# Small triangular inverses: two 64-row product stages put on either side of the second block's sliding-window values product

## The chip, the cores and the metric

The kernel runs on one core of a Trainium2 chip. The metric is the device time of one execution in microseconds (us). Before the change the median of three runs is 1251.22 us (1250.65 to 1251.36).

## What is computed

Two layers of a decoder trunk on 256 tokens of width 1024, all in fp32. In each layer three token mixers run on the same normalised input. The part that matters here is one step of the gated delta rule and, beside it, a sliding-window attention:

```python
def gated_delta_rule(q, k, v, g, beta):          # DN_HEADS = 4 heads of 128
    ...
    a = jnp.where(strict, jnp.einsum('bhncd,bhnsd->bhncs', k_beta, k) * decay, 0.0)
    t_mat = a + jnp.eye(C, dtype=f32)
    sol = lax.linalg.triangular_solve(t_mat, rhs, left_side=True, lower=True, unit_diagonal=True)
    ...

def sliding_window_attention(q, k, v, sinks):    # WINDOW = 128, two blocks of 128 tokens
    ...
    p = jnp.exp(s - m)
    p = p / (p.sum(-1, keepdims=True) + jnp.exp(sink - m))
    o = jnp.einsum('bnhgqk,bnkhd->bnqhgd', p.astype(v.dtype), vb)
```

After the mixers come a projection of each branch, gates, a common output projection and feed-forward stages. All of these are large matrix products whose weights (some 250 MB) stream in from memory once.

## The kernel before

**Weights.** Every weight piece of 128 x 1024 (`unit`, L110) is fetched by SyncE into a `raw` buffer (four of them), rounded by ScalarE into `whi` (a CAST) and completed by VectorE, which writes the remainder `wlo` (`split`, L125). A large product is then three TensorE matmuls (`mm3`: high by high, high by low, low by high), 128 x 512 each. There are five `whi` and five `wlo` buffers. A scheduler puts the casts at a priority of 300 instructions ahead of their place in the program.

**The small inverses.** Instead of a triangular solve the kernel inverts the two 128-row blocks (c = 0, 1) of each head by doubling: 16-row inverses on GpSimd, then `doubling` (L982 on) makes 32-row and 64-row inverses in four steps, each a group of small matmuls and a few copies on ScalarE, VectorE or GpSimd. `double` runs one step for both blocks. Two further stages make the 128-row inverse: `lower_products` (eight 64 x 64 matmuls, two ScalarE copies L1046 and L1047 into `TM`, in the trace `w`) and `upper_products` (eight 64 x 64 matmuls that read those copies, then two ScalarE multiplications L1056 into the inverse `Y`). The next user of `Y` is `rec_v0`, four 128 x 128 matmuls.

**Sliding attention.** `w_scores(tb, hh)` makes the scores and the softmax of block tb and half hh of the heads (ScalarE: L857, four exponentials L860, four multiplications L863). For the second block (tb = 1) the result must be turned. `w_leave(hh)` does this with two VectorE transposes each (L893, into `u` for hh = 0, into `bB` for hh = 1) and four GpSimd-issued DMAs to memory (L896, `tw`). `w_back` fetches it back with four GpSimd DMAs (L906, into two `pt` buffers, one for each 128 keys, each filled by one DMA of hh = 0 and one of hh = 1). `w_values(1)` multiplies both `pt` with the values: its first matmul waits for both DMAs into the first `pt`, its third for both into the second.

**What sets the order.** Large and small work is interleaved by hand with `weave` (after the n-th step of a large product, call these functions). TensorE's instructions in this part are kept in program order. ScalarE, VectorE and GpSimd are ordered by the scheduler from priorities and `issue_after` links, and at run time each executes its list strictly as it stands. The part at hand occurs once in each layer: `gates(1)`, eight steps with the doubling between them, then `branch(1)`, the projection of the sliding branch, four products of twelve matmuls.

Of the kernel before, what the change touches and what calls it, by code (L numbers as in the profile page):

```python
# [32 lines left out]
MAGIC = 0x5F3759DF  # L33
AHEAD = 300
HOLD = 4


@with_exitstack
def tile_trunk(ctx, tc, x, xT, mem, memT_, wst, lnp, memln, cvw, rows, cst, out):
    nc = tc.nc  # L40
# [21 lines left out]
    def T(pool, shape, tag, dt=F32, bufs=None):  # L62
        pool = pn if pool is pu and tag in NEAR else pool
        kw = {} if bufs is None else {"bufs": bufs}
        return pool.tile(shape, dt, tag=tag, name=nm(tag), **kw)

    def acc():
        return T(psA, [P, 512], "acc")

    def at():  # L70
        return T(psT, [P, 512], "at")

    def sm():
        return T(psS, [P, 512], "sm")
# [29 lines left out]
    def unit(w=U, dst=None, cuts=1, behind=None, parts=1):  # L104
        ahead = tc.high_priority(offset=AHEAD) if pos[0] >= 8 * P * U else nullcontext()
        raw = T(praw, [P, U], "raw")
        src = wst[pos[0]:pos[0] + P * w].rearrange("(p w) -> p w", p=P)
        pos[0] += P * w
        (ph, th), (pl, tl) = dst or ((phi, "whi"), (plo, "wlo"))
        with ahead:  # L110
            hi = T(ph, [P, U], th, F32R)
            lo = T(pl, [P, U], tl, F32R)
            for i in range(cuts):
                c = slice(i * w // cuts, (i + 1) * w // cuts)
                nc.sync.dma_start(raw[:, c], src[:, c])  # L115
                with ExitStack() as held:
                    for b in behind if isinstance(behind, tuple) else (behind,) if behind else ():
                        held.enter_context(tc.issue_after(b))
                    for j in range(c.start, c.stop, (c.stop - c.start) // parts):
                        e = slice(j, j + (c.stop - c.start) // parts)  # L120
                        newest[:] = split(hi[:, e], lo[:, e], raw[:, e])
        return hi, lo

    def split(hi, lo, src):
        return nc.scalar.copy(hi, src).ins, nc.vector.tensor_tensor(lo, src, hi.bitcast(F32), op=ALU.subtract).ins  # L125
# [3 lines left out]
    def pe(ins):  # L129

        return tc.keep_in_program_order(ins) if pinned[0] else ins

    def matmul(*a, **k):
        return pe(nc.tensor.matmul(*a, **k))  # L134
# [4 lines left out]
    def mm3(o, l, r, first, last, skip=False):  # L139
        (lh, ll), (rh, rl) = l, r  # L140
        matmul(o, lh, rh, start=first, stop=False, skip_group_check=skip)
        matmul(o, lh, rl, start=False, stop=False, skip_group_check=skip)
        matmul(o, ll, rh, start=False, stop=last, skip_group_check=skip)

    def weave(work, steps):

        for n, _ in enumerate(work, 1):
            for f in steps.get(n, ()):
                f()
# [410 lines left out]
    def mixers(l, hT, mkT, mv_, post0, post):  # L560
# [65 lines left out]
        def held(f):  # L626
            with ExitStack() as st:
                for b in late.values():
                    st.enter_context(tc.issue_after(b))
                f()  # L630
# [102 lines left out]
        TM = [T(pu, [P, 2, 4, P], f"w{2 + c}") for c in range(2)]  # L733
        AK = [T(pu, [P, 4, 2, P], f"u{12 + c}") for c in range(2)]
# [173 lines left out]
        def w_values(tb):  # L908
            if not oS:
                oS.extend(T(pu, [P, 4, S], tag, F32R) for tag in ("u6", "u7"))  # L910
            ts = slice(tb * P, (tb + 1) * P)
            pso = at()
            for kb in range(tb + 1):
                for kv in range(2):
                    hs = slice(kv * 64, kv * 64 + 64)
                    o, w = pso[hs].rearrange("p (y i x) -> p y i x", y=8, i=2), wpT[tb][kb].rearrange("p h (a i v x) -> p (h a) i v x", a=4, i=2, v=2)[:, :, :, kv]
                    matmul(o, swv[:, kb, hs], w, start=kb == 0, stop=kb == tb)
            for y in range(2):
                split(*(t[:, 2 * y:2 * y + 2, ts].rearrange("p i (a x) -> p i a x", a=4) for t in oS), pso[:, y * S:y * S + S].rearrange("p (a i x) -> p i a x", a=4, i=2))
# [42 lines left out]
        X64, X32, Y32 = (W[:, a:b].rearrange("p (c h i) -> p c h i", c=2, h=4) for a, b in ((0, 512), (512, 768), (768, 1024)))  # L962
        Y = T(pu, [P, 2, 4, P], "w1")
# [62 lines left out]
        stages = [doubling(c) for c in (1, 0)]  # L1026

        def double():
            for d in stages:
                next(d)  # L1030

        up, dn = slice(0, 64), slice(64, P)

# [5 lines left out]

        def lower_products():  # L1040

            pa, pb = (sm().rearrange("p (h c) -> p h c", h=4) for _ in range(2))
            for h in range(4):
                matmul(pa[dn, h, up], AK[0][up, h, 0, dn], X64[up, 0, h], start=True, stop=True)
                matmul(pb[up, h, dn], AK[1][dn, h, 0, up], Y[dn, 1, h, dn], start=True, stop=True)
            nc.scalar.copy(TM[0][dn, 1, :, up], pa[dn, :, up])  # L1046
            nc.scalar.copy(TM[1][up, 1, :, dn], pb[up, :, dn])  # L1047

        def upper_products():

            pa, pb = (sm().rearrange("p (h c) -> p h c", h=4) for _ in range(2))
            for h in range(4):
                matmul(pa[up, h, dn], TM[0][dn, 1, h, up], Y[dn, 0, h, dn], start=True, stop=True)
                matmul(pb[up, h, dn], X64[up, 1, h], TM[1][up, 1, h, dn], start=True, stop=True)
            for c, ps in enumerate((pa, pb)):
                nc.scalar.mul(Y[up, c, :, dn], ps[up, :, dn], -1.0)  # L1056

        def begin_inverse():

# [97 lines left out]
        def branch(n, o):  # L1157
            us = [unit(behind={1: late.get("pairs"), 2: fin.get("landed")}.get(n) if i > 1 else None) for i in range(4)]
            if not mg:
                mg.extend(T(pu, [P, D], f"u{4 + tb}") for tb in range(2))  # L1160
            gt = gts[n]
            for tb in range(2):
                ts = slice(tb * P, (tb + 1) * P)
                for j in range(2):
                    js = slice(j * 512, (j + 1) * 512)
                    ps = acc()
                    for k, (hi, lo) in enumerate(us):
                        mm3(ps, (o[0][:, k, ts], o[1][:, k, ts]), (hi[:, js], lo[:, js]), k == 0, k == 3)
                        if (n, tb, j, k) == (1, 0, 1, 2):
                            upper_products()  # L1170
                            w_values(1)
                    dst = gt[tb] if n else mg[tb]
                    late["dve"] = nc.vector.scalar_tensor_tensor(dst[:, js], gt[tb][:, js], 1.0, ps, op0=ALU.add, op1=ALU.mult).ins
                    if n:
                        with tc.issue_after(late["back"]):
                            nc.gpsimd.tensor_tensor(mg[tb][:, js], mg[tb][:, js], gt[tb][:, js], op=ALU.add)
                    yield
# [15 lines left out]
            4: [lambda: held(lambda: w_leave(1)), w_back],  # L1193
            5: [double],
            7: [double, lambda: w_values(0), lambda: held(land_v)],
            8: [lower_products, lambda: held(leave_q)]})
        weave(branch(1, oS), {
            2: [rec_v0],
            3: [rec_s1, lambda: held(land_q)],
# [51 lines left out]
    ps = sm()  # L1251
# [14 lines left out]
    for l in range(NL):  # L1266
        mT = []
        mid = memory_T(mT, l)
        if l == 0:

            mid[2] = lambda: load(cs, cst)
            more = {4: lambda *a: xres(0), 6: lambda *a: xres(1), 8: lambda *a: small()}
        post = Post(lnp[l, 0, 0], lnp[l, 0, 1], bounce=True)
        f1.rest(hT, 4, [((pu, "u0"), (pu, "u1")), ((pu, "u2"), (pu, "u3"))], post, mid, ends, {} if l else more)
        kv = memory_kv(mT, post)
        if l == 0:
            nc.scalar.activation(nea, rw[:, :, 8:12], AF.Exp)
            nc.vector.tensor_scalar(nea, nea, -1.0, None, ALU.mult)
        post2 = Post(lnp[l, 1, 0], lnp[l, 1, 1])
        mixers(l, post.hT, *kv, post, post2)  # L1280
        f2 = Ffn()
        begin(f2, post2.hT)
        last = l == NL - 1
        post = Post(lnp[l, 2, 0], lnp[l, 2, 1], last)
        f2.rest(post2.hT, 6, [((pu, a), (pu, b)) for a, b in (("u0", "u1"), ("u2", "u3"), ("u4", "u5"), ("u6", "u13"))], post, behind=post2.end)
        ends = post.end
        if not last:
            f1, hT = Ffn(), post.hT
            begin(f1, hT)
# [87 lines left out]
```

## Time and profile before

| | us |
|---|---|
| median of three runs | 1251.22 |
| the profiled execution | 1249.48 |
| its span (first to last instruction) | 1247.3 |
| TensorE busy within the span | 1236.5 |
| VectorE busy | 887.6 |
| ScalarE busy | 655.4 |
| GpSimd busy | 271.5 |

The profiled execution is 1.74 us below the median of the three runs, and 2.2 us of it lie around the span. TensorE works nearly without a pause, so the kernel gets longer or shorter by what TensorE waits for, or by what it executes; the other engines and the DMA queues count only where TensorE has to wait for them. Two stretches matter, 361 to 371 us in the first layer and 978 to 988 us in the second: they are the same instructions 617.3 us apart.

### The profile page before, as it was taken

The numbers are of one execution on the slowest core, as the hardware profiler recorded it, in microseconds if no ns is written. First come the engines' busy times: TensorE is split into PE (matmuls) and PEld (weight loads), VectorE is DVE, ScalarE is ACT, GpSimd is POOL, SyncE is SP. The second block draws the span as 40 slices with busy tenths as digits, with TensorE's granted clock in tenths as the row PEclk, the third lists the DMA queues.
The fourth block names the chain that finished last, engine by engine and source line by source line (L and its number), as shares of the span: only waits on it lengthen the run. The fifth ranks groups of instructions, "written<-read, shape, count | busy, mean of one in ns | idle before, by whom it ended". The sixth has DMA issues, their size and how long they took to land.

```text
span 1247.3 us, 18730 instructions
## 1 busy us (share of the span) xinstructions
PE 1236.5 (99%) x6812; PEld 1052.6 (84%) x6812; DVE 887.6 (71%) x1316; ACT 655.4 (53%) x976; POOL 271.5 (22%) x481
## 2 busy tenths in 40 slices
PE   9999999999999999999999999999999999999997
PEld 6888889999878888888888888899988788888886
DVE  6688567887768876665676665769869688666555
ACT  6456545656665544444455554456657644454541
POOL 1232102003751102221012220020046411122100
PEclk9999999999999999999999999999999999999999
DMA  8988866755675848886668886676566566688771
GB/s 296 320 267 279 259 228 202 239 171 179 184 242 169 269 140 257 240 242 220 220 207 241 262 255 216 215 238 207 170 192 214 177 215 213 204 243 240 242 230 74
DMA packets 83275, 276.73 MB, mean 222 GB/s; under 512 B 13776, under 2 KB 15216, under 8 KB 83184
## 3 DMA queue, kind: packets, MB, share of 16 engines
q1 hardware_dynamic: 66320, 232.40, 58.0%
q0 software_dynamic: 16720, 43.02, 12.0%
q8 instruction: 53, 0.87, 0.3%
q14 instruction: 38, 0.31, 0.1%
q10 hardware_dynamic: 144, 0.13, 0.0%
HBM read 253.77 MB, written 21.73 MB: 221 GB/s over the span
## 4 chain that ended last, share of the span: by engine, by line
PE 99%; DMA 0%; DVE 0%; SPq 0%; issue 0%; ACT 0%; DVEq 0%
PE acc L134 88%; PE at L134 4%; PE sm L134 3%; PE sm L137 1%; PE acc L332 1%; PE acc L333 1%; PE acc L335 1%; DMA raw<-in_wst_dram 0%; PE at L137 0%; DVE h L291 0%; DVE h L296 0%; SPq L115 0%; SPq L78 0%; ACT whi L125 0%; DVE bnst L277 0%
## 5 line engine op out<-in xcount | busy, mean ns | idle before, releaser
L125 DVE TENSOR_TENSOR wlo<-raw,whi 128x1024 fp32r<-128x1024 f32 (+2 forms) x405 | 486.4, 1209 | 252.1 <-ACT whi L125 249.7
L125 ACT CAST whi<-raw 128x1024 fp32r<-128x1024 f32 (+2 forms) x405 | 413.4, 1029 | 379.7 <-PE acc L134 293.6
L134 PE MATMUL acc<-whi,hT 128*128 128x512 f32 (+1 forms) x1824 | 559.9, 385 | 0.7 <-ACT whi L125 0.7
L134 PEld LDWEIGHTS acc<-whi,hT 128*128 128x128 f32 x1824 | 339.9, 188 | 70.1 <-ACT whi L125 2.7
L134 PE MATMUL acc<-wlo,hT 128*128 128x512 f32 (+1 forms) x912 | 350.1, 384 | 0.0
L134 PE MATMUL acc<-whi,u 128*128 128x512 f32 x812 | 259.0, 392 | 0.0
L134 PEld LDWEIGHTS acc<-wlo,hT 128*128 128x128 f32 x912 | 171.3, 188 | 32.9 <-DVE wlo L125 0.8
L134 PEld LDWEIGHTS acc<-whi,u 128*128 128x128 f32 x812 | 152.3, 188 | 33.8 <-issue 1.6
L362 POOL DMA_DIRECT2D tr<-t x176 | 96.0, 552 | 307.8 <-DVE t L356 307.6
L134 PE MATMUL acc<-wlo,u 128*128 128x512 f32 x406 | 158.2, 390 | 0.0
L134 PE MATMUL acc<-hT,whi 128*128 128x256 f32 x672 | 121.8, 284 | 0.0
L134 PEld LDWEIGHTS acc<-hT,whi 128*128 128x128 f32 x672 | 104.7, 192 | 0.0
L134 PE MATMUL acc<-hT,wlo 128*128 128x256 f32 x336 | 95.1, 283 | 0.0
L134 PEld LDWEIGHTS acc<-wlo,u 128*128 128x128 f32 x406 | 76.3, 188 | 15.5
L363 POOL DMA_DIRECT2D pt<-tr x44 | 24.6, 558 | 197.1 <-DMA tr<-t 143.0
L134 PEld LDWEIGHTS acc<-hT,wlo 128*128 128x128 f32 x336 | 64.4, 192 | 0.0
L353 ACT ACTIVATE t<-acc 128x256 f32<-128x256 f32 x88 | 33.4, 379 | 37.3 <-PE acc L134 37.2
L134 PE MATMUL acc<-u,u 128*128 128x512 f32 x186 | 46.4, 394 | 0.0
L354 DVE TENSOR_TENSOR t<-t,acc 128x256 f32<-128x256 f32 x88 | 36.7, 417 | 8.1 <-ACT t L353 3.8
L134 PEld LDWEIGHTS acc<-u,u 128*128 128x128 f32 x186 | 34.6, 188 | 7.5
L125 DVE TENSOR_TENSOR u<-pt,u 128x512 fp32r<-128x512 f32 x46 | 30.3, 659 | 13.2 <-ACT u L125 13.2
L125 ACT CAST u<-pt 128x512 fp32r<-128x512 f32 x46 | 28.1, 611 | 21.3 <-DMA pt<-tr 12.3
(264 smaller groups left out, 1190.4 us busy)
## 6 DMA issues: line engine op xcount, KB each, us to landing
raw<-in_wst_dram SPq DMA_DIRECT2D x409, 512.0 KB, 4.5
tr<-t POOLq DMA_DIRECT2D x176, 64.0 KB, 3.9
pt<-tr POOLq DMA_DIRECT2D x44, 256.0 KB, 5.2
raw<-in_wst_dram SPq DMA_DIRECT2D x16, 324.0 KB, 4.4
gB<-in_lnp_dram SPq DMA_DIRECT2D x6, 512.0 KB, 6.0
bB<-in_lnp_dram SPq DMA_DIRECT2D x6, 512.0 KB, 6.2
pt<-tw POOLq DMA_DIRECT2D x12, 256.0 KB, 5.6
tn<-pp POOLq DMA_DIRECT2D x16, 128.0 KB, 4.1
```

What stands on the lines that cost most here:

```text
L125: return nc.scalar.copy(hi, src).ins, nc.vector.tensor_tensor(lo, src, hi.bitcast(F32), op=ALU.subtract).ins
L134: return pe(nc.tensor.matmul(*a, **k))
L137: return pe(nc.tensor.transpose(*a))
L332: nc.tensor.matmul(ps, hT[0][:, k, ts], hi[:, c], start=k == 0, stop=False)
L333: nc.tensor.matmul(ps, hT[0][:, k, ts], lo[:, c], start=False, stop=False)
L335: nc.tensor.matmul(ps, hT[1][:, k, ts], hi[:, c], start=False, stop=k == KD - 1)
L353: act = nc.scalar.activation(t[:, :, tb, :], g, AF.Silu).ins
L354: ins = nc.vector.tensor_tensor(t[:, :, tb, :], t[:, :, tb, :], u, op=ALU.mult).ins
L362: nc.gpsimd.dma_start(d[:, :, q].rearrange("b c x -> c b x"), z[32 * q:32 * q + 32].rearrange("c (b x) -> c b x", b=4))
L363: back = nc.gpsimd.dma_start(y, d.rearrange("b c q x -> (b c) (q x)")).ins
```

## The change

The two 64-row stages are moved. `lower_products` was called after the last step of `gates(1)`; `upper_products` and then `w_values(1)` were called within the second product of `branch(1)`, before its last three matmuls. Now the order at that second place is `lower_products`, `w_values(1)`, `upper_products`, and nothing of them stands behind `gates(1)`. Apart from that, all steps of `double` and both stages get a scheduler priority of 120 instructions ahead. No instruction is added or removed.

```diff
+SOON = 120
...
         def double():
-            for d in stages:
-                next(d)
+            with tc.high_priority(offset=SOON):
+                for d in stages:
+                    next(d)
...
         def lower_products():
 
-            pa, pb = (sm().rearrange("p (h c) -> p h c", h=4) for _ in range(2))
...
+            with tc.high_priority(offset=SOON):
+                pa, pb = (sm().rearrange("p (h c) -> p h c", h=4) for _ in range(2))
...
         def upper_products():
 
-            pa, pb = (sm().rearrange("p (h c) -> p h c", h=4) for _ in range(2))
...
+            with tc.high_priority(offset=SOON):
+                pa, pb = (sm().rearrange("p (h c) -> p h c", h=4) for _ in range(2))
...
                         if (n, tb, j, k) == (1, 0, 1, 2):
+                            lower_products()
+                            w_values(1)
                             upper_products()
-                            w_values(1)
...
-            8: [lower_products, lambda: held(leave_q)]})
+            8: [lambda: held(leave_q)]})
```

TensorE's list around `w_values(1)` in the first layer. `sm` of 64x64 are the two stages, `at<-pt` is `w_values(1)`, `acc` is the large product. Before, the upper stage, the values and the large product:

```order
L134 MATMUL sm_3877<-w_469_2587,w_459_2575 64x64
L134 MATMUL sm_3878<-w_460_2576,w_468_2586 64x64
L134 MATMUL at_3889<-pt_3639,swv_2065 64x512 x2
L134 MATMUL at_3889<-pt_3640,swv_2065 64x512 x2
L134 MATMUL acc_3867<-whi_3847,u_655_3767 128x512
```

Now, the lower stage, the values and the upper stage:

```order
L135 MATMUL sm_3865<-w_468_2586,u_461_2577 64x64
L135 MATMUL sm_3866<-w_469_2587,u_462_2578 64x64
L135 MATMUL at_3877<-pt_3639,swv_2065 64x512 x2
L135 MATMUL at_3877<-pt_3640,swv_2065 64x512 x2
L135 MATMUL sm_3886<-w_469_2587,w_459_2575 64x64
L135 MATMUL sm_3887<-w_460_2576,w_468_2586 64x64
```

The lower stage has moved 21 large matmuls later, from ahead of `branch(1)` to ahead of the values, and the upper stage has moved behind the values.

The new priority also reorders ScalarE and VectorE earlier, within `gates(1)`. ScalarE's list there in the first layer: CAST `whi` are the four weight pieces of `branch(1)` (the names of one list are not those of the other), `pp_3496` is the softmax of the second block's second half, COPY `w` are copies of the doubling. Before, from the first weight cast on:

```order
L125 CAST whi_3829<-raw_3828 128x1024
L860 ACTIVATE pp_3496,sums_3508<-pp_3496,mx_3507 128x256 x2
L1154 ACTIVATE gt_3439<-acc_3441 128x512
L1019 COPY w_468_2586<-w_468_2586 32x4x32
L125 CAST whi_3835<-raw_3834 128x1024
L863 ACTIVATE pp_3496<-pp_3496,sums_3508 128x256 x4
L1008 COPY w_460_2576<-sm_3665 32x4x32 x2
L1008 COPY w_459_2575<-sm_3676 32x4x32 x2
L125 CAST whi_3841<-raw_3840 128x1024
```

Now, from the first weight cast on:

```order
L126 CAST whi_3817<-raw_3816 128x1024
L861 ACTIVATE pp_3496,sums_3508<-pp_3496,mx_3507 128x256 x4
L126 CAST whi_3823<-raw_3822 128x1024
L1009 COPY w_460_2576<-sm_3665 32x4x32 x2
L1009 COPY w_459_2575<-sm_3676 32x4x32 x2
L864 ACTIVATE pp_3496<-pp_3496,sums_3508 128x256 x3
L126 CAST whi_3829<-raw_3828 128x1024
L864 ACTIVATE pp_3496<-pp_3496,sums_3508 128x256
```

Ahead of these rows the four copies from the second doubling step, formerly spread behind them, now stand around the softmax's first small exponential (L858); the last of the four multiplications of `pp_3496` now stands behind the third weight cast instead of ahead of it.

VectorE's list at the same place, where `wlo` are the remainders of those weights and `bB` the two transposes of `w_leave(1)`. Before:

```order
L125 TENSOR_TENSOR wlo_3830<-raw_3828,whi_3829 128x1024
L861 TENSOR_TENSOR sums_3508<-sums_3508,sk_3509 128x4
L862 RECIPROCAL sums_3508<-sums_3508 128x4
L125 TENSOR_TENSOR wlo_3836<-raw_3834,whi_3835 128x1024
L893 STREAM_TRANSPOSE bB_3631<-pp_3496 128x512 x2
L656 TENSOR_TENSOR u_392_2081<-u_392_2081,kn_2083 128x512
```

Now:

```order
L126 TENSOR_TENSOR wlo_3818<-raw_3816,whi_3817 128x1024
L862 TENSOR_TENSOR sums_3508<-sums_3508,sk_3509 128x4
L863 RECIPROCAL sums_3508<-sums_3508 128x4
L126 TENSOR_TENSOR wlo_3824<-raw_3822,whi_3823 128x1024
L126 TENSOR_TENSOR wlo_3830<-raw_3828,whi_3829 128x1024
L894 STREAM_TRANSPOSE bB_3631<-pp_3496 128x512 x2
L657 TENSOR_TENSOR u_392_2081<-u_392_2081,kn_2083 128x512
```

The two transposes now stand behind the third weight remainder instead of the second. On GpSimd the eight copies of the second doubling step (L1023) now stand ahead of the four DMAs of `w_leave(0)`; the rest of its list keeps its order, and SyncE's list is unchanged. The second layer's lists show the same moves.

## Rows read from the trace of the kernel before

**Rows 1.** The page: busy us, share of the span, instructions.

```profile
PE 1236.5 (99%) x6812; PEld 1052.6 (84%) x6812; DVE 887.6 (71%) x1316; ACT 655.4 (53%) x976; POOL 271.5 (22%) x481
```

**Rows 2.** Timeline, TensorE, first layer: start us, us, engine, line, operation, [idle before].

```profile
361.22 0.39 PE L134 MATMUL acc<-whi,hT 128*128 128x512 f32 x1
361.54 0.68 PE L134 MATMUL sm<-w,u 64*64 64x64 f32 x16
362.15 0.50 PE L134 MATMUL acc<-whi,u 128*128 128x512 f32 x1
362.49 0.39 PE L134 MATMUL acc<-wlo,u 128*128 128x512 f32 x1
362.72 0.62 PE L134 MATMUL acc<-whi,u 128*128 128x512 f32 x2
...
367.14 0.68 PE L134 MATMUL sm<-w,w 64*64 64x64 f32 x16
367.75 1.94 PE L134 MATMUL at<-pt,swv 128*64 128x512 f32 x8
```

**Rows 3.** Timeline, TensorE, second layer: the same values product.

```profile
985.07 1.94 PE L134 MATMUL at<-pt,swv 128*64 128x512 f32 x8
```

**Rows 4.** Timeline, ScalarE, first layer.

```profile
345.92 0.21 ACT L857 ACTIVATE sk<-sk 128x4 f32<-128x4 f32 x1 [0.32 <-DVE sk L856]
346.68 0.60 ACT L1154 ACTIVATE gt<-acc 128x512 f32<-128x512 f32 x1 [0.56 <-PE acc L134]
...
348.73 1.04 ACT L125 CAST whi<-raw 128x1024 fp32r<-128x1024 f32 x1
349.66 0.51 ACT L860 ACTIVATE pp<-pp,mx 128x256 f32<-128x256 f32 x1
...
352.27 1.70 ACT L863 ACTIVATE pp<-pp,sums 128x256 f32<-128x256 f32 x4
354.00 1.09 ACT L1008 COPY w<-sm 32x128 f32<-32x128 f32 x4
...
356.19 0.92 ACT L1019 COPY w<-w 32x128 f32<-32x128 f32 x3
...
367.85 0.65 ACT L1056 ACTIVATE w<-sm 64x256 f32<-64x256 f32 x2 [3.54 <-PE sm L134]
```

**Rows 5.** Timeline, VectorE, first layer.

```profile
345.13 0.70 DVE L893 STREAM_TRANSPOSE u<-pp 128x512 f32<-128x512 f32 x1
...
346.43 1.18 DVE L125 TENSOR_TENSOR wlo<-raw,whi 128x1024 fp32r<-128x1024 f32 x1
...
347.60 0.48 DVE L999 TENSOR_TENSOR w<-w,sm 128x128 f32<-128x128 f32 x2
348.00 0.49 DVE L1000 STREAM_TRANSPOSE w<-w 128x128 f32<-128x128 f32 x2
...
354.00 1.31 DVE L893 STREAM_TRANSPOSE bB<-pp 128x512 f32<-128x512 f32 x2 [0.38 <-ACT pp L863]
```

**Rows 6.** Timeline, GpSimd: the last two fetches of `w_back`, first and second layer.

```profile
363.25 1.06 POOL L906 DMA_DIRECT2D pt<-tw  x2 [3.74 <-DMA tw<-bB]
...
980.32 1.06 POOL L906 DMA_DIRECT2D pt<-tw  x2 [3.49 <-DMA tw<-bB]
```

**Rows 7.** By line, issue to landing: L896 into tw<-bB; L906, first and second layer.

```profile
DMA to landing us min/median/max: 2.9/4.2/5.4
...
DMA to landing us min/median/max: 3.7/3.9/4.1
...
DMA to landing us min/median/max: 3.5/3.8/4.2
```

**Rows 8.** By stretches: stretch, length, PE, PEld, DVE, ACT, POOL busy, PEclk, DMA, GB/s.

```profile
1238.00:1240.00 2.00, 1.09 (x10) 0.89 (x8) 0.90 (x3) 0.00 (x0) 0.00 (x0) 1.00 0.00 0
1240.00:1242.00 2.00, 0.00 (x0) 0.00 (x0) 1.90 (x7) 0.29 (x1) 0.00 (x0) 0.85 0.00 0
```

**Rows 9.** Timeline, TensorE, start of the kernel: its first four matmuls.

```profile
1.52 3.78 PE L1253 MATMUL sm<-pp 128*128 128x512 f32 x4 [1.52 <-DVE pp L1250]
```

More of the change, by code (lines that the diff above doesn't have):

```diff
@@ L1040, in lower_products @@
         def lower_products():
-            pa, pb = (sm().rearrange("p (h c) -> p h c", h=4) for _ in range(2))
[L1043 to L1047, printed above, removed]
-        def upper_products():
-            pa, pb = (sm().rearrange("p (h c) -> p h c", h=4) for _ in range(2))
[L1052 to L1056, printed above, removed]
+            with tc.high_priority(offset=SOON):
+                pa, pb = (sm().rearrange("p (h c) -> p h c", h=4) for _ in range(2))
+                for h in range(4):
+                    matmul(pa[dn, h, up], AK[0][up, h, 0, dn], X64[up, 0, h], start=True, stop=True)
+                    matmul(pb[up, h, dn], AK[1][dn, h, 0, up], Y[dn, 1, h, dn], start=True, stop=True)
+                nc.scalar.copy(TM[0][dn, 1, :, up], pa[dn, :, up])
+                nc.scalar.copy(TM[1][up, 1, :, dn], pb[up, :, dn])
+        def upper_products():
+            with tc.high_priority(offset=SOON):
+                pa, pb = (sm().rearrange("p (h c) -> p h c", h=4) for _ in range(2))
+                for h in range(4):
+                    matmul(pa[up, h, dn], TM[0][dn, 1, h, up], Y[dn, 0, h, dn], start=True, stop=True)
+                    matmul(pb[up, h, dn], X64[up, 1, h], TM[1][up, 1, h, dn], start=True, stop=True)
+                for c, ps in enumerate((pa, pb)):
+                    nc.scalar.mul(Y[up, c, :, dn], ps[up, :, dn], -1.0)
         def begin_inverse():
```

## The prediction

> **What bounds the kernel now.** I read the page first, then TensorE's timeline around the moved stages, then the lists of ScalarE, VectorE and GpSimd that feed them. The page says that TensorE is busy 1236.5 us of 1247.3 [rows 1]. So the question is only what TensorE executes and what it waits for. In the timeline of the first layer [rows 2] the lower stage runs straight after the last large matmul, and the upper stage and the values product follow each other without a hole: the upper stage starts at 367.14, the values at 367.75, and the lower stage takes the same 0.61 us (361.54 to 362.15). TensorE waits for nothing here. But one of its inputs comes late: the last two fetches into `pt` are issued at 363.25 and about 363.8 [rows 6] and land 3.7 and 4.1 us later [rows 7], at 366.95 and 367.9. TensorE wants the first at 367.75 [rows 2] and the second about 0.95 later (half of the product's 1.94). The slack is 0.8 us in each case. In the second layer the fetches land at 980.32 + 3.5 = 983.82 and 980.85 + 4.2 = 985.05 [rows 6, 7], and the values start at 985.07 [rows 3]: a slack of 1.25 us for the first and 0.97 for the second. This small slack is what the change will meet.
>
> **What the move itself saves.** A 64-row stage between large matmuls costs more than its own 0.61 us. From the large matmul ahead to the stage it is 0.32 us, and the first large matmul behind holds the next up by 0.34, where two large matmuls normally follow each other at 0.23 (the 0.62 of a pair less one matmul's 0.39) [rows 2]. The lower stage therefore costs 0.32 + 0.61 + 0.34 - 2 x 0.23 = 0.81 us. Beside the values, which already pay for coming and going, it costs its 0.61. The move saves 0.20 us in each layer, 0.40 in all. It also makes TensorE arrive at the values 0.81 us earlier: `lower_products` has left its place ahead of `branch(1)`, and at the values it takes the place and the 0.61 us of `upper_products`.
>
> **The new waits in TensorE's list.** `upper_products` reads what ScalarE copies from `lower_products`. Those two copies take about as long as the two of L1056, 0.65 us, and can start some 0.71 us after the stage's start (367.85 against 367.14) [rows 2, 4]; they end 1.36 us after it, while the values alone occupy TensorE for 0.61 to 2.48 us after it. The values hide them; without that cover they would cost 0.75. Behind the upper stage stand three large matmuls (0.34 + 0.23 + 0.23) and then `rec_v0`, which reads `Y`: it is due 1.41 us after the upper stage's start, and the multiplications end 1.36 us after it. That just fits. I take it at 0 and keep 0.2 us per layer for the range. In ScalarE's list the cast of the values' first half stands ahead of those multiplications, but its input is ready before theirs.
>
> **What the priorities delay.** This is the larger part. The transposes into `bB` are the source of the late fetches: they end at 354.00 + 1.31 = 355.31, then come GpSimd's `tw` writes (up to 5.4 us to land), then the two fetches [rows 5 to 7]. In the new lists they need the fourth multiplication of `pp`, which stands behind the third weight cast, and they stand behind that cast's remainder on VectorE. I follow the new lists through the first layer with the durations of the rows. VectorE: the first transpose from 345.13 (0.70), the two L999 (0.48), the remainder (1.18), the two L1000 (0.49) [rows 5], so the first L1000 ends at about 347.7. ScalarE: the tanh of L1154 still waits for TensorE and ends at 347.28 [rows 4]. Then two copies from 347.7 at 0.31 each (0.92 for three): 348.3. The small exponential, 0.21: 348.5. Two more copies: 349.15. The first weight cast, whose successor starts 0.93 later: 350.1. Four exponentials at 0.51: 352.1. The second cast, 0.93: 353.05. Four copies, 1.09: 354.15. Three of the four multiplications, 1.28: 355.4. The third cast, 1.04: 356.45 [rows 4]. VectorE: the remainder, 1.18, to 357.65; the two transposes, 1.31, to 358.95 [rows 5]. That is 3.6 us later than before. GpSimd is free by then (its eight copies and four writes moved ahead of that time), so the whole chain of writes and fetches shifts by these 3.6 us. The weights themselves are not late: the third and fourth are read only when TensorE reaches the third and fourth quarter of a product that starts after 361. Both layers have the same lists, so I take 3.6 for each.
>
> **The sum.** First layer: the first `pt` lands at 366.95 + 3.6 = 370.55; TensorE arrives at 367.75 - 0.81 = 366.94. It waits 3.6 us; the second `pt`, at 371.5, is due then at the same moment as it lands. Second layer: 983.82 + 3.6 = 987.42 against 984.26, 3.16 us; the second `pt` lands at 988.65 against 988.37, another 0.28: 3.44 together. The waits add up to 7.05 us; less the 0.40 saved, 6.65. Nothing later gives this back, since TensorE's 99% leave no wait to absorb it.
>
> **The clock.** A wait of this length may cost once more. At the end of the kernel TensorE's last matmul ends at about 1239.1, and the granted clock, 1.00 until then, has a mean of 0.85 from 1240 to 1242 [rows 8]; between 1.00 and 0.50 (2.4 and 1.2 GHz) that puts its fall at 1241.4, 2.3 us after the work stopped. The Trainium skill states the same direction, that inactivity brings the throttle back (TensorE: Matmul & The Clock Gate, Part 1: The HAM clock gate). At the start the first four matmuls take 3.78 us [rows 9], 0.85 or more each, where four pairs of the values product with the same 512 columns take 1.94 [rows 2]: the clock is low for at least 3.8 us of work. If it falls 2.3 us into a wait of 3.5 and stays low for 3.8, some 2.6 us of work run at half speed, a loss of 1.3 us. No row shows a wait of this length between matmuls, so this is bounded by 0 and 3.8 / 2 = 1.9 us for each layer. I take one fall in the two layers, 1.3 us, because the wait is longer than 2.3 us but not by much.
>
> On the profiled execution, 1249.48 + 6.65 + 1.3 = 1257.4; it lies 1.74 below the median, so the median goes to **1259.2 us**.
>
> **The rivals.** *Not slower: quick transfers.* The price of the delay hangs on what `tw` and `pt` need to land. Of the four `tw` writes the quickest landed in 2.9 us, the slowest in 5.4 [rows 7]; in the new order they are issued later, when perhaps fewer weight transfers are under way. With 2.9 for the last write the chain is 2.5 us shorter: waits of 1.1 and 0.95 us, no fall of the clock, 2.05 - 0.4 = 1.65 more, 1252.9: no difference that can be told. It decides if the last write lands in under 3.6 us or so. Against it: the weight fetches are released by the same remainders at nearly the same times as before. The Trainium skill gives such a GpSimd-issued transfer about 2.0 us and its bytes over 436 GB/s (DMA: Bandwidth & Descriptors, Anatomy of one DMA); the estimate from that page is 2.3 us for a write of 128 KB and 2.6 for a fetch of 256 KB, by which `pt` would land ahead of TensorE and the sum would be only the 0.4 saved, 1250.8. The rows' 5.4 and 3.7 speak against that, since DMA engines are shared with the weights. *Only the move counts.* If the fourth multiplication and the transposes turn out not to gate the fetches, 1251.22 - 0.4 = 1250.8, also within the noise. Against it: the idle time of GpSimd ahead of the fetches ends with the `tw<-bB` writes [rows 6]. *Worse.* The clock falls in both layers with 1.9 each and `rec_v0` waits 0.2 each: 6.65 + 3.8 + 0.4, 1262.1.
>
> **How the numbers follow.** The forecast, both layers wait for `pt` and the clock falls at most once: 0.62 (1256 to 1260.5). Clock falls in both layers or transfers land later: 0.16 (1260.5 to 1263). Quick transfers: 0.15, of which 0.04 still over 0.2%. Only the move: 0.07, of which 0.03 for a gain that I do not see. A measurement of this kernel tells about 0.2%, 2.5 us, from no change. That gives slower 0.82, same 0.15, faster 0.03. The range leaves out the worst of the third case and most of the last two: 1254.5 to 1262.5.
>
> **What would show it.** In the profile after: a hole in TensorE of some 3.5 us just ahead of `at<-pt` in both layers, released by the DMA `pt<-tw`; the `bB` transposes ending 3.6 us later relative to the stages around them; the lower stage without a gap ahead of that hole; no wait of the upper stage on ScalarE. A granted clock below 1.00 in the stretches behind the holes shows the clock term. The prediction is wrong if the fetches land in time, if ScalarE reaches the fourth multiplication earlier than at about 356, or if `branch(1)` starts late for a weight or for the first block's values.

## The result and the profile after

| | before | after |
|---|---|---|
| median of the runs made side by side, us | 1250.93 (1249.10 to 1251.36) | 1260.01 (1259.07 to 1262.34) |
| ratio to before, 95% interval | | 1.0081 (1.0068 to 1.0093) |
| the profiled execution, us | 1249.48 | 1259.07 |
| its span, us | 1247.3 | 1257.0 |

The kernel got slower by 0.8%, some 9 to 10 us, where 1259.2 was forecast. TensorE's time by cause of waiting (us in total, times, longest) has one entry of that size, where before had none at this place:

```profile
PE at L135 <- DMA pt<-tw: 7.5, 2, 3.8
```

TensorE's timeline shows the two places. First layer, answering [rows 2] (start us, us, engine, line, operation, [idle before and what ended it]):

```profile
366.49 0.68 PE L135 MATMUL sm<-w,u 64*64 64x64 f32 x16
370.87 1.94 PE L135 MATMUL at<-pt,swv 128*64 128x512 f32 x8 [3.69 <-DMA pt<-tw]
372.74 0.68 PE L135 MATMUL sm<-w,w 64*64 64x64 f32 x16
373.35 0.50 PE L135 MATMUL acc<-whi,u 128*128 128x512 f32 x1
...
374.15 1.05 PE L135 MATMUL sm<-u,w 128*128 128x128 f32 x8
374.96 0.47 PE L135 MATMUL acc<-whi,u 128*128 128x512 f32 x1
```

Second layer, answering [rows 3]:

```profile
987.15 0.68 PE L135 MATMUL sm<-w,u 64*64 64x64 f32 x16
991.59 3.68 PE L135 MATMUL at<-pt,swv 128*64 128x512 f32 x8 [3.76 <-DMA pt<-tw]
995.20 1.12 PE L135 MATMUL sm<-w,w 64*64 64x64 f32 x16
996.25 0.79 PE L135 MATMUL acc<-whi,u 128*128 128x512 f32 x1
...
997.35 1.05 PE L135 MATMUL sm<-u,w 128*128 128x128 f32 x8
998.16 0.47 PE L135 MATMUL acc<-whi,u 128*128 128x512 f32 x1
```

From the lower stage's start to the values' start 0.61 us would be enough; it takes 370.87 - 366.49 = 4.38 and 991.59 - 987.15 = 4.44. The waits cost 3.77 and 3.83, together 7.6 us. In the second layer the values product itself takes 3.68 instead of 1.94, and from its start to the large matmul behind `rec_v0` it is 6.57 us, against 4.09 in the first layer: another 2.48 us. With the 0.4 us that the move saves, 7.6 + 2.48 - 0.4 = 9.7, the difference of the spans.

The source, as it stands in VectorE's timeline, answering [rows 5]: the `bB` transposes now end at 359.02 instead of 355.31.

```profile
356.57 1.23 DVE L126 TENSOR_TENSOR wlo<-raw,whi 128x1024 fp32r<-128x1024 f32 x1 [2.17 <-ACT whi L126]
357.72 1.30 DVE L894 STREAM_TRANSPOSE bB<-pp 128x512 f32<-128x512 f32 x2
```

ScalarE's timeline, answering [rows 4], shows why: the third weight cast, and only then the last of the four multiplications that the transposes need.

```profile
355.51 1.03 ACT L126 CAST whi<-raw 128x1024 fp32r<-128x1024 f32 x1
356.45 0.50 ACT L864 ACTIVATE pp<-pp,sums 128x256 f32<-128x256 f32 x1
```

And GpSimd, answering [rows 6]: the last two fetches are issued at 366.94 instead of 363.25, 3.69 us later.

```profile
359.31 2.31 POOL L897 DMA_DIRECT2D tw<-bB  x4 [7.04 <-DVE bB L894]
...
366.94 1.07 POOL L907 DMA_DIRECT2D pt<-tw  x2 [4.22 <-DMA tw<-bB]
...
988.08 1.07 POOL L907 DMA_DIRECT2D pt<-tw  x2 [4.36 <-DMA tw<-bB]
```

The second layer by stretches of 2 us (stretch, length, busy time of PE, PEld, DVE, ACT, POOL, then PEclk, the granted clock as a share of 2.4 GHz, DMA share, GB/s), the view of [rows 8]:

```profile
988.00:990.00 2.00, 0.00 (x0) 0.00 (x0) 0.00 (x0) 0.59 (x2) 1.85 (x4) 1.00 0.92 291
990.00:992.00 2.00, 0.41 (x2) 0.33 (x4) 0.00 (x0) 0.00 (x0) 1.01 (x1) 0.53 0.61 227
992.00:994.00 2.00, 2.00 (x6) 0.54 (x4) 0.00 (x0) 0.00 (x0) 1.26 (x3) 0.50 0.00 0
994.00:996.00 2.00, 2.00 (x18) 0.80 (x16) 0.28 (x1) 0.37 (x1) 0.97 (x2) 0.50 0.20 8
996.00:998.00 2.00, 2.00 (x16) 1.70 (x14) 0.59 (x2) 0.90 (x3) 0.00 (x0) 0.77 0.02 4
998.00:1000.00 2.00, 2.00 (x12) 1.70 (x11) 0.58 (x2) 0.59 (x1) 1.29 (x1) 1.00 0.00 0
```

And the wait of the first layer in the same view:

```profile
368.00:370.00 2.00, 0.00 (x0) 0.00 (x0) 0.00 (x0) 0.00 (x0) 1.80 (x3) 1.00 0.89 293
370.00:372.00 2.00, 1.13 (x6) 0.54 (x8) 0.00 (x0) 0.00 (x0) 0.15 (x1) 1.00 0.18 69
```

In the second layer TensorE stands still from 987.8 on. Its clock is at the upper level (1.00, 2.4 GHz) for 2.3 us of that, drops to 0.50 (1.2 GHz) at 990.1 and comes back at 996.9. These two moments follow from the means 0.53 and 0.77, and the trace's own record of the clock has them at 990.11 and 996.94. In the first layer the clock stays at 1.00 through a wait of almost the same length. The profiled execution is the shortest of the four, with a mean granted clock of 0.996 over its span; the other three have 0.993 to 0.994, so one fall need not be the usual case. Their traces were not taken.

### The profile page after: what moved, and what is told of

Read it like the earlier page. It is cut to its first block, busy times and chain, and to the rows that moved or that the text cites. A ratio compares the mean times of both kernels' runs of the same rounds, so it can differ in the third digit from the quotient of the medians.

```text
span 1257.0 us, 18726 instructions
## 1 busy us (share of the span) xinstructions
PE 1239.1 (99%) x6812; PEld 1054.5 (84%) x6812; DVE 886.0 (70%) x1316; ACT 655.4 (52%) x976; POOL 271.3 (22%) x481
## 4 chain that ended last, share of the span: by engine, by line
PE 90%; DMA 3%; DVE 2%; POOL 2%; issue 1%; ACT 1%; SPq 0%; DVEq 0%; POOLq 0%; ACTq 0%
PE acc L135 81%; PE at L135 3%; PE sm L135 2%; DMA raw<-in_wst_dram 1%; PE sm L138 1%; PE acc L333 1%; PE acc L334 1%; PE acc L336 1%; DMA tw<-bB 1%; DVE wlo L126 1%; POOL t L954 1%; DMA pt<-tw 1%; DMA w<-dr 0%; ACT whi L126 0%; POOL t L955 0%
```

## The experiments

Theory: the priority on `double` delays the `bB` transposes, so the fetches, so the values product; and where TensorE stands still that long its clock falls and some work behind runs at half speed. Rival: the new place of the two 64-row stages makes the cost. The runs below share chips and runs of before in two groups; the median of before is 1249.95 us in the first (`move_only`, `double_prio`, `fill`, `leave80`) and 1249.75 in the second. Ratios are to before; 0.001 is 1.25 us.

**The move alone** (`move_only`): the stages stand where the change puts them, no priority is raised.

```diff
-            with tc.high_priority(offset=SOON):
+            with nullcontext():
```

(at all three places)

> The stages stand where the change puts them, no priority is raised. Theory (the delayed transposes make the cost): the bB transposes end near 355.3 as before, the first pt lands near 366.95, TensorE arrives at the values 0.81 earlier (366.94) and waits 0 to 0.15 us in each layer; the clock stays at 1.00 until the end; 1250.9 - 0.4 + 0.1 = about 1250.6. Rival (the place of the stages makes the cost): holes of 3.5 us or more ahead of the values as in the changed kernel, about 1260.

Measured: 1251.26 us, ratio 1.0009 (1.0000 to 1.0018). The rival's 1260 is out: the place of the stages makes little of the cost, about a tenth. But the theory's gain of 0.3 did not come either; the ratio says a loss of about 1 us, though its interval begins at no loss at all. TensorE's timeline of the first layer shows where one can come from:

```profile
360.88 0.39 PE L135 MATMUL acc<-whi,hT 128*128 128x512 f32 x1
361.69 0.50 PE L135 MATMUL acc<-whi,u 128*128 128x512 f32 x1 [0.41 <-ACT u L126]
...
364.02 0.73 PE L135 MATMUL acc<-whi,u 128*128 128x512 f32 x2 [0.20 <-DVE u L126]
...
367.86 1.08 PE L135 MATMUL at<-pt,swv 128*64 128x512 f32 x4
369.71 1.08 PE L135 MATMUL at<-pt,swv 128*64 128x512 f32 x4 [0.77 <-DMA pt<-tw]
```

Two things that were covered before are bare in this execution. At the start of `branch(1)` the split of the first block's values (`u`) is late by 0.4 and 0.2 us; the lower stage used to lie over it. (In the changed kernel, whose lower stage is gone from there too, `branch(1)` starts in the first layer without such a wait, at 361.64.) And the second `pt` lands 0.8 us after TensorE wants it. In this execution the transposes ended at 356.16, 0.85 us later than in before, while TensorE was 0.34 earlier (360.88 against 361.22 for the last matmul of `gates(1)`, [rows 2]). The lists are the same: a weight cast on ScalarE waited 2.13 us for its weight's DMA and started at 339.42, in before 0.91 and 338.58. The whole list behind it shifted. The 0.81 us by which TensorE now arrives earlier at the values were the slack that would have taken up most of that.

**The priority alone, on `double`** (`double_prio`): the stages back at their old places, their priorities off, so that TensorE's list is that of before.

```diff
-            with tc.high_priority(offset=SOON):
+            with nullcontext():
                 pa, pb = (sm().rearrange("p (h c) -> p h c", h=4) for _ in range(2))
...
+                            upper_products()
-                            lower_products()
                             w_values(1)
-                            upper_products()
...
-            8: [lambda: held(leave_q)]})
+            8: [lower_products, lambda: held(leave_q)]})
```

(the first of these edits in both stages)

> Only the steps of double get the priority; the two 64-row stages stand where they stood before. Theory: the bB transposes end near 359, pt lands as late as in the changed kernel (370.7 and 987.4 + 4.0), TensorE arrives 0.81 later than there, so the waits are 3.77 - 0.81 = 2.96 and 3.83 - 0.81 = 3.02, 6.0 together: 1250.9 + 6.0 = 1256.9 if the clock stays at 1.00, 1259.4 if it falls once (2.5 each). Rival (the place of the stages makes the cost): waits under 0.3 us, about 1250.9.

Measured: 1259.79 us, ratio 1.0072 (1.0058 to 1.0085). So this one priority brings the loss by itself. TensorE's timeline, both layers, and VectorE's transposes:

```profile
366.59 0.68 PE L135 MATMUL sm<-w,w 64*64 64x64 f32 x16
370.53 3.68 PE L135 MATMUL at<-pt,swv 128*64 128x512 f32 x8 [3.26 <-DMA pt<-tw]
...
990.15 0.68 PE L135 MATMUL sm<-w,w 64*64 64x64 f32 x16
993.94 3.38 PE L135 MATMUL at<-pt,swv 128*64 128x512 f32 x8 [3.11 <-DMA pt<-tw]
```

```profile
356.93 1.30 DVE L894 STREAM_TRANSPOSE bB<-pp 128x512 f32<-128x512 f32 x2
```

The waits cost 3.94 - 0.61 = 3.33 and 3.79 - 0.61 = 3.18, a little more than the 3.0 expected. The clock fell not once but in both layers: both values products are slow, though both waits are shorter than the two of the changed kernel. By stretches (columns as above):

```profile
371.00:373.00 2.00, 2.00 (x6) 0.54 (x4) 0.00 (x0) 0.00 (x0) 1.46 (x3) 0.50 0.05 2
375.00:377.00 2.00, 2.00 (x11) 1.82 (x11) 1.10 (x3) 0.37 (x1) 0.40 (x1) 0.63 0.00 0
```

```profile
994.00:996.00 2.00, 2.00 (x6) 0.67 (x8) 0.00 (x0) 0.00 (x0) 1.07 (x2) 0.57 0.00 1
996.00:998.00 2.00, 2.00 (x6) 0.69 (x3) 0.24 (x1) 0.37 (x1) 1.15 (x3) 0.57 0.14 8
```

Since TensorE's list is that of before, each matmul can be set against itself. The values start 2.78 us later than in [rows 2] in the first layer and 8.87 later than in [rows 3] in the second; of the 6.09 between them 3.18 are the second wait, and 2.9 the price of the first fall. The second fall came after work had resumed and was shorter (0.50 from 994.3 to 997.7); over it the matmuls, each set against itself in before, lose 1.66 us. A fall thus has no one price here.

**The wait filled** (`fill`): the changed kernel, with matmuls added between the lower stage and the values.

```diff
-        def w_values(tb):
+        def w_values(tb, fill=None):
...
+            if fill:
+                for _ in range(15):
+                    matmul(pso, *fill, start=True, stop=True)
...
-                            w_values(1)
+                            w_values(1, (o[0][:, 0, ts], us[0][0][:, js]))
```

> The changed kernel with 15 added 128x512 matmuls between the lower stage and the values (work that is thrown away, about 15 x 0.23 = 3.4 us), so that TensorE is busy for most of the time in which it otherwise waits. Theory (the clock fell because TensorE stood still): pt lands as in the changed kernel, the added matmuls and what is left of the wait last 3.8 us together in each layer, the values product takes 1.94 in both layers, the granted clock stays at 1.00: 1250.9 - 0.4 + 7.6 = about 1258.1, 1.9 to 2.5 under the changed kernel although it executes more. Rival (the fall has another cause, or costs nothing at the end): 1260.0 with a values product of 3.7 in one layer.

Measured: 1257.89 us, ratio 1.0060 (1.0047 to 1.0072): 0.0021 or 2.6 us less than the changed kernel's ratio, for 30 matmuls more (the two intervals just overlap). TensorE's timeline of the first layer and the values of the second, then the second layer's stretches:

```profile
366.69 0.68 PE L135 MATMUL sm<-w,u 64*64 64x64 f32 x16
367.30 3.70 PE L135 MATMUL at<-whi,u 128*128 128x512 f32 x15
371.25 1.94 PE L135 MATMUL at<-pt,swv 128*64 128x512 f32 x8 [0.25 <-DMA pt<-tw]
...
992.18 1.94 PE L135 MATMUL at<-pt,swv 128*64 128x512 f32 x8
```

```profile
988.00:992.00 4.00, 4.00 (x31) 3.09 (x28) 0.25 (x1) 0.73 (x2) 2.81 (x4) 1.00 0.85 291
992.00:996.00 4.00, 3.94 (x33) 2.33 (x33) 0.77 (x2) 1.27 (x4) 2.22 (x4) 1.00 0.05 6
```

The clock stays at 1.00 and both products take 1.94. The other executions agree: all five of `fill` have a mean clock of 0.998 or 0.999, all four of the changed kernel 0.993 to 0.996. So the fall came from TensorE's standing still, and its price is a real part of the loss: about 2.5 us of the 9 to 10.

**Half of the wait filled** (`fill7`): 7 instead of 15 added matmuls.

```diff
-                for _ in range(15):
+                for _ in range(7):
```

> The changed kernel with 7 instead of 15 added 128x512 matmuls between the lower stage and the values (their products are thrown away): 7 x 0.23 = 1.6 us of the wait are filled, some 2.1 us are left in each layer. Theory (in the two records in which the clock fell ahead of the values it fell 2.3 and 2.4 us after TensorE had stopped, so a wait of 2.1 mostly ends before that): pt lands as in the changed kernel, values products of 1.94 in both layers, the clock at 1.00: as with 15, about 1257.9. Rival (any wait beyond about 1 us brings the fall): values products of 3.4 to 3.7 in a layer, 2.5 us more for each, 1260.4 or 1262.9.

Measured: 1257.61 us, ratio 1.0063 (1.0050 to 1.0076). In the profiled execution (1256.55) waits of 1.23 and 1.92 us are left, and the values take 1.98 and 1.94: no fall.

```profile
370.61 1.98 PE L135 MATMUL at<-pt,swv 128*64 128x512 f32 x8 [1.23 <-DMA pt<-tw]
...
991.50 1.94 PE L135 MATMUL at<-pt,swv 128*64 128x512 f32 x8 [1.92 <-DMA pt<-tw]
```

The median is as forecast. The rival's "any wait beyond about 1 us" is out. But the five executions go from 1255.78 to 1260.11, and the two longest (1259.37, 1260.11) lie 2 us or more above the others' middle at a mean clock of 0.997, against 0.999 and 0.998 in the two shortest; the median execution has 0.997 too. That may be a fall in one layer; their traces were not taken, so it stays open whether a wait of this length is always safe.

**The transposes brought forward again** (`leave80`): the changed kernel, and a higher priority for what the fetches hang on.

```diff
-            late["act"] = [nc.scalar.mul(pr[:, h, :nk], pr[:, h, :nk], sums[:, h:h + 1]) for h in range(4)][-1].ins
+            with (tc.high_priority(offset=LEAVE) if (tb, hh) == (1, 1) else nullcontext()):
+                late["act"] = [nc.scalar.mul(pr[:, h, :nk], pr[:, h, :nk], sums[:, h:h + 1]) for h in range(4)][-1].ins
...
-            4: [lambda: held(lambda: w_leave(1)), w_back],
+            4: [lambda: leave_soon(lambda: held(lambda: w_leave(1))), w_back],
```

(`LEAVE` is 80, `leave_soon` calls its argument at that priority)

> The changed kernel, but the four multiplications of the second softmax half and the two bB transposes are raised by 80 instructions, so that in the lists the multiplications stand ahead of the doubling's copies and of the third weight cast, and the transposes ahead of the third remainder. Theory: the transposes end near 356.15 instead of 359.0, pt lands 2.85 us earlier, waits of 0.9 (first layer) and 0.4 to 1.0 us (second), no fall of the clock: 1250.9 - 0.4 + 1.3 to 1.9 = about 1252. Rival (the wait hangs on something else, as on the eight doubling copies ahead of the writes of w_leave(0) on GpSimd, or on TensorE's earlier arrival alone): waits of 3.5 us remain, about 1260.

Measured: 1251.80 us, ratio 1.0010 (1.0002 to 1.0019). With everything else of the change in place, most of the loss is gone. VectorE's transposes in the first layer, then TensorE's values in both:

```profile
354.21 1.30 DVE L896 STREAM_TRANSPOSE bB<-pp 128x512 f32<-128x512 f32 x2 [0.39 <-ACT pp L866]
```

```profile
367.02 1.08 PE L136 MATMUL at<-pt,swv 128*64 128x512 f32 x4 [0.48 <-DMA pt<-tw]
369.19 1.08 PE L136 MATMUL at<-pt,swv 128*64 128x512 f32 x4 [1.09 <-DMA pt<-tw]
...
985.35 2.22 PE L136 MATMUL at<-pt,swv 128*64 128x512 f32 x8 [0.18 <-DMA pt<-tw]
```

The transposes end at 355.51 and the clock never falls. The eight doubling copies ahead of the writes of `w_leave(0)`, which are still there, are no cause. What is left are 1.8 us of short waits at the values; the profiled execution of the move alone has 1.4 us of them, at the values and at the split.

**Can the move be had without those waits?** Two kernels without the change's priorities, in which the four multiplications stand ahead of the second weight cast, the transposes ahead of the second remainder, and the split of the first block's values a little earlier. In `move_best` the stages stand where the change puts them, in `leave_only` where they were.

```diff
+LEAVE = 110
+VAL = 100
...
-            with tc.high_priority(offset=SOON):
+            with nullcontext():
...
-            7: [double, lambda: w_values(0), lambda: held(land_v)],
+            7: [double, lambda: val_soon(lambda: w_values(0)), lambda: held(land_v)],
```

(and the two edits of `leave80`; `val_soon` calls its argument at the priority `VAL`)

> The move without the change's priorities, and the sources of the two inputs that came late in the run with the move alone brought forward in the lists: the four multiplications of the second softmax half ahead of the second weight cast, the bB transposes ahead of the second remainder, and the split of the first block's values ahead of the doubling's last copy and of two reductions. Theory (the move alone lost because it spent the slack of the fetches and uncovered that split): bB transposes end about 0.95 earlier, near 354.4, no wait at the values, at most 0.3 us at the start of branch(1): the move's 0.4 shows at last, 249.95 + 1000 - 0.4 + 0.1 = about 1249.7 where before is 1249.95. Rival (the move costs something of its own that no wait shows): about 1251.3, as with the move alone.

> The same inputs brought forward, but the two 64-row stages stay where they were before. Theory: TensorE waited for neither input before, so nothing is gained: 1249.95 within 0.1%, 0.2 to 0.4 us above the kernel with the move. Rival (bringing them forward delays weights, or the slack of before was often overdrawn): 1 us or more off 1249.95.

Measured: 1250.56 us, ratio 1.0006 (0.9997 to 1.0015), and 1249.42, ratio 0.9998 (0.9989 to 1.0007). `leave_only` came out as forecast: no difference. `move_best` did not: its 0.4 us gain does not show, and it lies 1.1 us above its counterpart (the intervals overlap). VectorE, GpSimd and TensorE of `move_best`, first layer:

```profile
353.62 1.31 DVE L897 STREAM_TRANSPOSE bB<-pp 128x512 f32<-128x512 f32 x2 [1.83 <-ACT pp L867]
```

```profile
363.60 1.06 POOL L910 DMA_DIRECT2D pt<-tw  x2 [4.17 <-DMA tw<-bB]
```

```profile
366.22 0.68 PE L137 MATMUL sm<-w,u 64*64 64x64 f32 x16
367.68 1.94 PE L137 MATMUL at<-pt,swv 128*64 128x512 f32 x8 [0.78 <-DMA pt<-tw]
```

The wait at the start of `branch(1)` is gone. But the transposes ended at 354.93, 0.4 us earlier than in [rows 5], and yet the fetches were issued at 363.60, 0.35 later than in [rows 6]: this time the writes needed longer to land. In `leave_only`, first layer, transposes that end 0.63 earlier (354.68) bring the fetches forward by only 0.14 (363.11). So the rival's "cost of its own that no wait shows" is not needed: the wait of 0.78 us shows, more than the 0.4 saved. What failed is the expectation that an earlier issue means an earlier landing. Neither kernel beats the one before by what these runs can tell.

## Why the prediction was right, step by step

The forecast was 1259.2 us (1254.5 to 1262.5), the measured median is 1260.01. For the profiled execution the sum gave 1257.4, and it took 1259.07; the difference comes from two terms, the waits (0.55 us) and the clock (1.18). That the median came within 0.8 us is in part luck: the forecast carried over the 1.74 us by which the profile of before lies under its median, and the changed kernel's profile lies only 0.94 under its own.

- **The bound.** Right: all of the change in time stands in TensorE's waits and clock. Nothing behind gave it back.
- **The move's saving.** 0.20 us per layer as work: from the last matmul of `gates(1)` (361.42) to the large matmul behind the two stages (373.35) it is 11.93, less the wait of 3.77 is 8.16; before, the same work went from 361.22 [rows 2] to 369.62, 8.40. So 0.24. TensorE arrived at the values within about 0.2 us of when it was expected to, and neither the upper stage nor `rec_v0` waited.
- **The priorities.** Right nearly to the tenth. From the order of the lists and the durations of [rows 4, 5] the transposes were to end at 358.95; they ended at 359.02. The third cast was to end at 356.45, and the fourth multiplication follows at 356.45. `double_prio` and `leave80` show that this is the cause: the priority on `double` makes the loss without the move, and undoing the delay takes it away with the move in place.
- **The waits.** 7.05 forecast, 7.6 measured. The term was mis-sized in the second layer, 3.44 against 3.83. Transfer times of one execution were carried over to a tenth, while from the transposes' end to the fetches' issue it took 7.78 us in the second layer of before and 8.07 here; over the profiled runs it is 7.3 to 8.7.
- **The clock.** The mechanism was right, and once in two layers was right for this execution, the shortest of four; by their mean clocks of 0.993 to 0.994 (the profile of `double_prio`, with two falls, has 0.994) the others may have had two. The length of the wait did not decide it (no fall in 3.69 us, a fall in 3.11), so the count of one was a guess that this execution met. The size was not right: 1.3 us forecast, 2.48 measured, above even the upper bound of 1.9. The step that failed is the 3.8 us for which the low clock was to last, read from the kernel's start [rows 9] as a length that would hold anywhere. Those rows gave it as a least length ("at least 3.8 us of work"), and half of a least length is no upper bound. It was at 0.50 for 6.8 us, 5.35 of them over work, and half of that, 2.7, is near the 2.48 lost. The same holds in `double_prio`: 5.95 us of work at the low clock, 2.9 lost, and 3.4 us, 1.66 lost.
- **The rivals.** Quick transfers did not come: the writes and fetches took as long as before although they were issued 3.7 us later. The first fetch of the first layer needed from 366.94 to just before 370.87. The rows, not the estimate from the Trainium skill (DMA: Bandwidth & Descriptors, Anatomy of one DMA), had the right size. The worse case, a fall in both layers, is what `double_prio` showed in its profile. On the clock the Trainium skill's direction (TensorE: Matmul & The Clock Gate, Part 1: The HAM clock gate) agrees with `fill`: work in place of the wait kept the clock at 1.00.
- **"Only the move counts, 1250.8."** As a rival it lost because the transposes do gate the fetches. But its own price was wrong too: the move by itself did not gain 0.4, its median is 1.3 us above before, with an interval that begins at no loss. A slack of 0.8 us and an arrival 0.81 us earlier were taken to cancel; the slack is that of one execution, and what the lower stage covered at its old place, the split of the first block's values, had no price in it.

Of the change's parts, the priority on `double` makes the loss, and the move is worth nothing here. The priorities on the stages themselves were not tried apart.

## What to carry to other kernels

A priority is not given to a step, it is taken from what stands in the same lists: before raising one, look in each in-order list for what now stands behind, and whether the longest chain (here transposes, writes, fetches, values) starts there. A slack read from one execution is a reserve and not a gift: where the inputs come through shared DMA engines, moving the consumer forward by just the slack can buy waits. And a wait of some microseconds on TensorE can cost more than itself: in three of the four waits of 3.1 to 3.8 us traced here the clock fell, and each fall cost about half of the time for which it lay low over work (2.5, 2.9 and 1.7 us).

## What was not expected of the hardware

- The clock's fall does not follow from the length of the wait alone: it stayed at 1.00 through 3.69 us of idle time in the changed kernel's first layer, and fell in waits of 3.76, 3.26 and 3.11 us. In two of the three it fell 2.3 and 2.4 us after TensorE stopped, in the third only when work had resumed (994.3 against 993.94). It stayed at 0.50 for 6.8, 6.8 and 3.4 us.
- Writes that GpSimd issues earlier need not land earlier. Over the runs the stretch from the transposes' end to the fetches' issue varies by 1.4 us (7.3 to 8.7) with the same writes in it, more than the 0.4 and 0.6 us by which `move_best` and `leave_only` brought the transposes of the first layer forward. Which other transfers they share the DMA engines with at that moment was not taken apart.
- While TensorE waited in the second layer, VectorE had no work at all and ScalarE 0.59 us of two (988 to 990), and the DMA share fell from 0.92 to 0.00 within 4 us: the weight stream stopped too, presumably for want of free buffers. That left no longer waits for weights: TensorE waited 0.5 us in all for `whi` in the changed kernel, 0.7 in the kernel before.
